# Two-layer decoder trunk: six groups of the MLP through seven products, two plain, and up projections in 512- and 256-column passes

## The chip, the cores and the metric

The kernel runs on one core of a Trainium2 chip. The metric is the device time of one execution in microseconds; below "us" always means that.

## The reference, cut to what matters

The input is 256 positions of 2048 numbers (fp32). Two layers follow, each a token mixer and then an MLP, both behind an RMSNorm and added to the residual x. The change touches the MLP alone:

```python
def squared_relu_mlp(h, w_up, w_down):
    return jnp.square(jax.nn.relu(h @ w_up)) @ w_down
...
        h = rms_norm(x, mlp_norm[layer])
        x = x + squared_relu_mlp(h, w_up[layer], w_down[layer]).astype(x.dtype)
```

Here w_up is 2048 x 8192 and w_down is 8192 x 2048. The norm's scale per position is taken out of the MLP: since relu squared is homogeneous of degree two, the kernel multiplies the MLP's output by the squared scale (the tile rB) at the end.

## The kernel before, in words

**Precision.** Every fp32 operand is split into hi (rounded to the matmul's reduced format) and lo (the rest), and a product is hi by hi, hi by lo and lo by hi. ScalarE makes hi of a weight chunk (L1308) and VectorE lo (L1319), five and four chunks ahead of TensorE. Weights come from HBM in transfers of 1 MB into three buffers named raw, issued on SyncE's queue. The activations stand in the tile xs, for each of 16 K-tiles 256 columns of hi and 256 of lo side by side.

**One stream.** All weight chunks of the kernel are in one list, `stream`, and its order is the order of TensorE's work. A chunk is four K-tiles of 256 weight columns, thus 8 pairs of K-tile and 128-column half (j). A `Block` is the chunks that add up in one PSUM tile: it asks for the tile (`take`) at its first chunk and calls `done` after its last. In `consume` the kind says which passes are made: kind U makes three passes of 256 columns (L467 to L469) and adds everything in one bank; kind T, so far used by the mixers, makes one pass of 512 columns (hi of the weight by hi and lo of the activation, L476) and one of 256 (lo by hi, L477), and its result stands in two halves of two banks that `done` has to add.

**The MLP** (`mlp`) splits the 8192 hidden columns into NGRP = 8 groups of 1024. A group's up projection is nb = 4 blocks of 16 K-tiles. `up_done` empties the bank (relu L1002, square L1006) and leaves jobs that make the tile hs of it. The down projection of groups 0 to 6 goes "through products": for each of four column blocks cb of 512 columns, seven chunks make 29 products where 32 would be plain (seven products in place of eight for three of four block pairs, and the pair named in PLAIN the plain way). Each product is three passes of 256 columns (L497 to L499) into the PSUM tiles s0 and s1, two banks each. ScalarE copies s0 and s1 to the SBUF tile stage, of which there are two (L1116), and GpSimd's queue adds them by DMA to the DRAM tensor sums (L1119, L1121). The stream interleaves products of group g with the up chunks of group g + 1: in each round 7 product chunks (87 passes) and the 4 chunks of one up block, and an up block's end is followed by two product chunks (18 passes) before the next up block.

**The end of an MLP.** After the last round of products `combine` adds the eight quarters of sums among each other by DMA, one column block after the other (L1133), and loads the result to the tile sum (L1137), all on GpSimd's queue, which runs in order. The last group's down projection is plain: 8 blocks of 256 columns with 8 K-tiles each. Before the last chunk of block b `add_sums(b)` turns its part of sum (L1148), scales it and adds it to x; `down_done` adds the block itself (L1160, L1161). In the last layer block 7 has the kind "last", and `final_block` prepares the output block by block with the gain tile (L1232), which GpSimd's queue loads (L982).

**PSUM.** Eight banks: two for side, two each for s0 and s1, and one each for the two tiles named up that hold the U blocks.

## Time and profile before

| what | value |
|---|---|
| median of 3 runs | 2225.75 us (2218.46 to 2233.47) |
| the profiled execution, its own time | 2223.67 us |
| its span in the profile | 2221.9 us |
| TensorE, matmul passes | 2167.8 us busy, 16494 passes |
| TensorE, weight loads | 2087.0 us busy |
| VectorE | 1605.1 us busy |
| ScalarE | 1286.8 us busy |
| DMA | 468.14 MB, 211 GB/s over the span |

How to read it: the passes of TensorE overlap, so a busy TensorE tells only that one of them was in flight, and its rate has to be read from the number of passes in a stretch. The profiled execution took 2 us less than the median, so numbers from it carry over to the median as they are.

### The profile page before, as it was taken

The page shows a single profiled execution, that of the slowest core. Times are in us where ns is not written, and L with a number is a line of the kernel's source. Part 1 is how long each engine was busy: PE and PEld are TensorE (multiplying, and loading weights), DVE is VectorE, ACT ScalarE, POOL GpSimd, SP SyncE. Part 2 cuts the span into 40 slices and gives each one's busy share as a digit, 9 for nine tenths or more (in the row PEclk, how much of TensorE's full clock was granted, in tenths as well). Part 3 has the DMA queues.
Part 4 walks back from the last instruction along what each step waited for, and adds up shares of the span by engine and source line. Part 5 has one row for each costly group of instructions (what it writes and reads, how often), then busy time and mean ns, then how long its engine had stood idle before and what let it go on. Part 6 is the DMA issues. An engine that isn't in the chain of part 4 may idle for free.

```text
span 2221.9 us, 40179 instructions
## 1 busy us (share of the span) xinstructions
PE 2167.8 (98%) x16494; PEld 2087.0 (94%) x16494; DVE 1605.1 (72%) x2145; ACT 1286.8 (58%) x1746; POOL 176.9 (8%) x233
## 2 busy tenths in 40 slices
PE   9999999999999999999699999999999999999987
PEld 7898989999999999998688889989999999999986
DVE  6765666778787878777667665577887878787656
ACT  6554545566667666665355436456666666666552
POOL 0000000000000000023200000000000000000232
PEclk9999999999999999999899999999999999999998
DMA  8545456688989898899754455666788888889995
GB/s 261 175 147 162 152 188 177 193 253 232 244 243 237 248 236 232 236 251 236 186 171 152 142 174 167 162 177 191 245 242 239 238 246 244 238 238 244 249 240 140
DMA packets 307943, 468.14 MB, mean 211 GB/s; under 512 B 12120, under 2 KB 182176, under 8 KB 307760
## 3 DMA queue, kind: packets, MB, share of 16 engines
q1 hardware_dynamic: 280224, 392.32, 57.7%
q0 software_dynamic: 27504, 73.25, 16.3%
q8 instruction: 129, 2.11, 0.4%
q14 instruction: 54, 0.44, 0.1%
q10 hardware_dynamic: 32, 0.01, 0.0%
HBM read 404.73 MB, written 69.21 MB: 213 GB/s over the span
## 4 chain that ended last, share of the span: by engine, by line
issue 46%; PE 39%; DMA 10%; POOL 5%; DVE 0%; ACT 0%; POOLq 0%; SPq 0%; ACTq 0%
PE mm L476 14%; DMA sums<-sums 9%; PE mm L477 8%; POOL sums L1121 3%; PE mm L463 2%; PE mm L461 2%; PE mm L462 2%; PE up L467 2%; PE up L468 2%; PE up L469 2%; PE mm L479 1%; PE side L352 1%; DMA sums<-stage 1%; PE side L375 1%; PE side L421 1%
## 5 line engine op out<-in xcount | busy, mean ns | idle before, releaser
L1308 ACT ACTIVATE hi<-raw 128x1024 fp32r<-128x1024 f32 (+2 forms) x812 | 742.7, 930 | 557.2 <-PE up L468 252.1
L1319 DVE TENSOR_TENSOR lo<-raw,hi 128x1024 fp32r<-128x1024 f32 (+2 forms) x812 | 851.3, 1066 | 286.5 <-ACT hi L1308 104.9
L469 PE MATMUL up<-xs,lo 128*128 128x256 f32 x2048 | 577.3, 282 | 4.4 <-DVE lo L1319 4.4
L468 PE MATMUL up<-xs,hi 128*128 128x256 f32 x2048 | 578.7, 283 | 0.0
L467 PE MATMUL up<-xs,hi 128*128 128x256 f32 x2048 | 577.1, 282 | 1.6 <-DVE xT L758 1.6
L497 PE MATMUL s<-hi,hs 128*128 128x256 f32 x1624 | 456.2, 281 | 0.0
L498 PE MATMUL s<-lo,hs 128*128 128x256 f32 x1624 | 456.0, 281 | 0.0
L499 PE MATMUL s<-hi,hs 128*128 128x256 f32 x1624 | 456.0, 281 | 0.0
L469 PEld LDWEIGHTS up<-xs,lo 128*128 128x128 f32 x2048 | 386.7, 189 | 6.2 <-DVE lo L1319 6.2
L467 PEld LDWEIGHTS up<-xs,hi 128*128 128x128 f32 x2048 | 386.2, 189 | 1.9 <-ACT hi L1308 1.9
L468 PEld LDWEIGHTS up<-xs,hi 128*128 128x128 f32 x2048 | 384.5, 188 | 0.0
L476 PE MATMUL mm<-xs,hi 128*128 128x512 f32 x885 | 319.6, 401 | 1.6 <-DVE t L1160 1.0
L499 PEld LDWEIGHTS s<-hi,hs 128*128 128x128 f32 x1624 | 306.3, 189 | 0.0
L497 PEld LDWEIGHTS s<-hi,hs 128*128 128x128 f32 x1624 | 306.3, 189 | 0.0
L498 PEld LDWEIGHTS s<-lo,hs 128*128 128x128 f32 x1624 | 306.2, 189 | 0.0
L1319 DVE TENSOR_TENSOR lo<-w,hi 128x1024 fp32r<-128x1024 f32 x168 | 205.7, 1224 | 123.3 <-PE up L469 67.7
L477 PE MATMUL mm<-xs,lo 128*128 128x256 f32 x944 | 259.0, 280 | 0.2 <-DVE lo L1319 0.2
L476 PEld LDWEIGHTS mm<-xs,hi 128*128 128x128 f32 x885 | 166.1, 188 | 39.4 <-issue 1.2
L1308 ACT ACTIVATE hi<-w 128x1024 fp32r<-128x1024 f32 x168 | 176.9, 1053 | 37.8 <-DVE w L1068 27.8
L477 PEld LDWEIGHTS mm<-xs,lo 128*128 128x128 f32 x944 | 177.3, 188 | 3.0 <-DVE lo L1319 0.5
L1116 ACT ACTIVATE stage<-s 128x1024 f32<-128x1024 f32 x112 | 114.4, 1021 | 74.5 <-PE s L499 65.4
L1121 POOL DMA_DIRECT2D sums<-stage x96 | 89.1, 1006 | 848.1 <-ACT stage L1116 846.3
(297 smaller groups left out, 2761.7 us busy)
## 6 DMA issues: line engine op xcount, KB each, us to landing
raw<-w_up SPq DMA_DIRECT2D x128, 1024.0 KB, 6.2
raw<-w_down SPq DMA_DIRECT2D x128, 1024.0 KB, 5.5
sums<-stage POOLq DMA_DIRECT2D x112, 512.0 KB, 9.3
raw<-od_w_in SPq DMA_DIRECT2D x36, 1024.0 KB, 5.0
raw<-ev_w_in SPq DMA_DIRECT2D x30, 1024.0 KB, 5.4
raw<-ev_w_out SPq DMA_DIRECT2D x16, 1024.0 KB, 5.0
raw<-od_w_in SPq DMA_DIRECT2D x20, 512.0 KB, 4.9
sums<-sums POOLq DMA_DIRECT2D x64, 128.0 KB, 5.8
```

Source lines behind the costliest of these rows:

```text
L467: mm(ps[:, j], hi[:, n, c], m[:, 0:T], start=first and j == 0, stop=False)
L468: mm(ps[:, j], hi[:, n, c], m[:, T:], start=False, stop=False)
L469: mm(ps[:, j], lo[:, n, c], m[:, 0:T], start=False, stop=last and j == 1)
L476: mm(ps[:, j], hi[:, n, c], m, start=first, stop=False)
L477: mm(ps[:, j, 0:T], lo[:, n, c], m[:, 0:T], start=False, stop=False)
L497: mm(ps, x[:, a, 0:P], hi[:, w], start=(i, o) == bank[0], stop=False)
L498: mm(ps, x[:, a, 0:P], lo[:, w], start=False, stop=False)
L499: mm(ps, x[:, a, P:], hi[:, w], start=False, stop=(i, o) == bank[-1])
L1116: act(stage, ps.rearrange("p b c -> p (b c)"), AF.Copy)
L1121: nc.gpsimd.dma_start(to, stage, accum_op=OP.add)
L1308: act(d, r, AF.Copy)
L1319: tt(d, r, f32(h), op=OP.subtract)
```

## The change

The constant NS = 6 says how many groups go through products; groups 6 and 7 are plain. The up chunks of group 7 follow alone after the last round, and then come the 8 plain down blocks, now with 16 K-tiles each. `combine` starts after the products of group 5. Kind U is gone: up blocks and plain down blocks are of kind T, except the block of kind "last". A T block needs two banks, so there is one tile up (groups 1 to 6 use it, `take_up`), and the up blocks of groups 0 and 7 and the down blocks alternate between s0 and s1 (`take_free`). `up_done` and `down_done` first copy one half of the PSUM tile on ScalarE and add the other on VectorE. The sums of the column blocks 2 and 3 are loaded into the two buffers of stage.

```diff
--- before.py
+++ after.py
@@ -463,11 +463,7 @@
                 mm(o, xl, hi[:, n], start=False, stop=last)
                 continue
             c = slice(j * P, (j + 1) * P)
-            if block.kind == "U":
-                mm(ps[:, j], hi[:, n, c], m[:, 0:T], start=first and j == 0, stop=False)
-                mm(ps[:, j], hi[:, n, c], m[:, T:], start=False, stop=False)
-                mm(ps[:, j], lo[:, n, c], m[:, 0:T], start=False, stop=last and j == 1)
-            elif block.kind == "last":
+            if block.kind == "last":
                 mm(ps[j], hi[:, n, c], m[:, 0:T], start=first, stop=False)
                 mm(ps[j], hi[:, n, c], m[:, T:], start=False, stop=False)
                 mm(ps[j], lo[:, n, c], m[:, 0:T], start=False, stop=last)
@@ -982,7 +978,7 @@
                 nc.gpsimd.dma_start(fn[i], final_norm[c].unsqueeze(0).to_broadcast([P, D // 2]))
             E["fn"] = lambda c0, n: fn[c0 // (D // 2)][:, c0 % (D // 2):c0 % (D // 2) + n]
 
-        NGRP = 8
+        NGRP, NS = 8, 6
         PLAIN = (3,)
         W = FF // NGRP
         nb = W // T
@@ -991,15 +987,21 @@
         hs = {}
 
         def take_up():
-            return st["banks"].tile([P, 2, T], F32, name="up", bufs=2)
+            return banks("up", 1)
+
+        def take_free(b):
+            return lambda: banks(f"s{b % 2}", 1)
 
         def take_last():
-            return [banks(f"s{j}", 1)[:, 0, 0:T] for j in range(2)]
+            ps = banks("s1", 1)
+            return [ps[:, j, 0:T] for j in range(2)]
 
         def up_done(grp, b):
             def f(ps):
                 t = temp()
-                act(t, ps, AF.Relu)
+                act(t, ps[:, :, T:], AF.Copy)
+                tt(t, ps[:, :, 0:T], t, op=OP.add)
+                act(t, t, AF.Relu)
                 if (grp, b) != (0, 0):
                     need(("h", layer) + ((grp, b - 1) if b else (grp - 1, nb - 1)))
                 r = E["pool"].tile([P, 8, P], F32, name="hr", bufs=1)
@@ -1007,7 +1009,7 @@
 
                 def job():
                     h = E["pool"].tile([P, 7, 2 * P], F32R, name="hs", bufs=2 * nb)
-                    if grp == NGRP - 1:
+                    if grp >= NS:
                         h = h.rearrange("p o t -> p (o t)")[:, 0:4 * T].rearrange("p (j t) -> p j t", j=2)
                         split_into(h, r[:, 0:4].rearrange("p (j k) t -> p j (k t)", j=2))
                     elif b in PLAIN:
@@ -1119,7 +1121,7 @@
                     nc.gpsimd.dma_start(to, stage)
                 else:
                     nc.gpsimd.dma_start(to, stage, accum_op=OP.add)
-                if grp == NGRP - 2 and half == "s1":
+                if grp == NS - 1 and half == "s1":
                     jobs.spawn(combine(cb), keys=[("sum", cb)], delay=2)
                     if last and cb == 3:
                         load_gain()
@@ -1132,7 +1134,8 @@
                 for to, src in step:
                     nc.gpsimd.dma_start(to, src, accum_op=OP.add)
                 yield 2, 0
-            g = hs["sum", cb] = E["pool"].tile([P, 2, 2, T], F32, name="sum", bufs=2)
+            g = E["pool"].tile([P, 4 * T], F32, name="sum" if cb < 2 else "stage", bufs=2)
+            g = hs["sum", cb] = g.rearrange("p (a b c) -> p a b c", a=2, b=2)
             for tok, half, src in ((0, 0, p4), (0, 1, p7), (1, 0, p2), (1, 1, p3)):
                 nc.gpsimd.dma_start(g[:, tok, half], src)
             jobs.done.add(("sum", cb))
@@ -1157,7 +1160,9 @@
                 need(("rB", n0))
                 t = temp()
                 rB = E.setdefault("rB", st["rB"])
-                tt(t, ps, rB[:, None, :].to_broadcast([P, 2, T]), op=OP.mult)
+                act(t, ps[:, :, T:], AF.Copy)
+                tt(t, ps[:, :, 0:T], t, op=OP.add)
+                tt(t, t, rB[:, None, :].to_broadcast([P, 2, T]), op=OP.mult)
                 tt(xT[b], xT[b], t, op=OP.add)
                 if last:
                     final_block(E, b)
@@ -1180,8 +1185,8 @@
             return chunks
 
         def up_list(grp):
-            blocks = [Block("U", eights(up, grp * W + b * T, KT), mov, up_done(grp, b), take=take_up)
-                      for b in range(nb)]
+            blocks = [Block("T", eights(up, grp * W + b * T, KT), mov, up_done(grp, b),
+                            take=take_up if 0 < grp <= NS else take_free(b)) for b in range(nb)]
             return [(block, i) for block in blocks for i in range(len(block.chunks))]
 
         def product_list(grp):
@@ -1193,22 +1198,26 @@
             return [(block, i) for block in blocks for i in range(len(block.chunks))]
 
         stream.extend(up_list(0))
-        for grp in range(NGRP - 1):
+        for grp in range(NS):
             s, u = product_list(grp), up_list(grp + 1)
             for i in range(len(u)):
                 a, b = (i // 4 * 7 + (0, 2, 4, 5, 7)[i % 4 + e] for e in range(2))
                 stream.extend(s[a:b] + u[i:i + 1])
 
+        for grp in range(NS + 1, NGRP):
+            stream.extend(up_list(grp))
+
         def h_mov(kt):
-            need(("h", layer, NGRP - 1, kt // 2))
-            return hs[NGRP - 1, kt // 2][:, kt % 2]
-        wd = down[FF - W:]
+            grp, b = NS + kt // (2 * nb), kt // 2 % nb
+            need(("h", layer, grp, b))
+            return hs[grp, b][:, kt % 2]
+        wd = down[NS * W:]
         for b in range(8):
+            w = eights(wd, b * T, (NGRP - NS) * W // P)
             if last and b == 7:
-                add(Block("last", eights(wd, b * T, W // P), h_mov, lambda ps: last_block(E, ps), take=take_last,
-                          extra=add_sums(b)))
+                add(Block("last", w, h_mov, lambda ps: last_block(E, ps), take=take_last, extra=add_sums(b)))
             else:
-                add(Block("U", eights(wd, b * T, W // P), h_mov, down_done(b), take=take_up, extra=add_sums(b)))
+                add(Block("T", w, h_mov, down_done(b), take=take_free(b), extra=add_sums(b)))
         return open_pool, pool_ctx.close
 
 
@@ -1242,7 +1251,7 @@
             tt(t[:, j], ps[j], E["rB"], op=OP.mult)
             tt(xl[:, j], xl[:, j], t[:, j], op=OP.add)
             act(sq[:, j], xl[:, j], AF.Square)
-        sums, turn = banks("s0", 1), side()
+        sums, turn = banks("up", 1), side()
 
         def add_up(a, first, last):
             for tok in range(2):
```

In VectorE's order, where an up block ends between products (raw is a buffer of weights, w_7124 to w_7263 are weight tiles made for the products), the kernel before has these rows:

```order
L1319 TENSOR_TENSOR lo<-raw,hi 128x1024
L1319 TENSOR_TENSOR lo<-raw,hi 128x512
L1319 TENSOR_TENSOR lo<-raw,hi 128x1024
L1319 TENSOR_TENSOR lo<-w_7124,hi 128x1024
L1319 TENSOR_TENSOR lo<-w_7125,hi 128x1024
L1060 TENSOR_TENSOR w_7263<-raw 128x512
```

Nothing of the up block's end stands there, since before ScalarE alone empties the bank. In VectorE's order of the changed kernel the same place reads (w_6890 and w_6891 are made weight tiles again):

```order
L1328 TENSOR_TENSOR lo<-raw,hi 128x1024
L1328 TENSOR_TENSOR lo<-raw,hi 128x512
L1328 TENSOR_TENSOR lo<-raw,hi 128x1024
L1003 TENSOR_TENSOR t<-up,t 128x512
L1328 TENSOR_TENSOR lo<-w_6890,hi 128x1024
L1328 TENSOR_TENSOR lo<-w_6891,hi 128x1024
```

The addition t<-up,t now stands between the lo of the chunk three ahead and that of the chunk four ahead.

In ScalarE's order at this place (stage<-s copies s0 or s1, t<-up empties the up bank, hr<-t squares) the kernel before has:

```order
L1308 ACTIVATE hi<-raw 128x512
L1116 ACTIVATE stage<-s_6968 128x1024
L1308 ACTIVATE hi<-raw 128x1024
L1116 ACTIVATE stage<-s_7036 128x1024
L1308 ACTIVATE hi<-w_7124 128x1024
L1002 ACTIVATE t<-up 128x512
L1006 ACTIVATE hr<-t 128x512
```

The relu that empties the bank comes behind two staged copies and the hi of the chunk four ahead. ScalarE of the changed kernel has there:

```order
L1317 ACTIVATE hi<-raw 128x512
L1118 ACTIVATE stage<-s_6754 128x1024
L1317 ACTIVATE hi<-raw 128x1024
L1118 ACTIVATE stage<-s_6811 128x1024
L1317 ACTIVATE hi<-w_6890 128x1024
L1002 ACTIVATE t<-up 128x512
L1004 ACTIVATE t<-t 128x512
L1008 ACTIVATE hr<-t 128x512
```

One row more stands there: t<-up is now the copy of one half, and the relu, t<-t, comes behind it and waits for VectorE's addition.

In GpSimd's queue at the end of layer 0's products (sums_1_99 to sums_3_101 are the DRAM tensors of the column blocks 1 to 3) the kernel before has, following group 6:

```order
L1133 DMA sums_1_99<-sums_1_99 128x256 x6
L1121 DMA sums_2_100<-stage 128x1024 x2
L1133 DMA sums_1_99<-sums_1_99 128x256 x2
L1137 DMA sum<-sums_1_99 128x256 x4
L1133 DMA sums_2_100<-sums_2_100 128x256 x6
L1121 DMA sums_3_101<-stage 128x1024 x2
L1133 DMA sums_2_100<-sums_2_100 128x256 x2
L1137 DMA sum<-sums_2_100 128x256 x4
L1133 DMA sums_3_101<-sums_3_101 128x256 x8
L1137 DMA sum<-sums_3_101 128x256 x4
```

The staged copies of block 2 stand behind six additions of block 1, those of block 3 behind six of block 2. In GpSimd's queue of the changed kernel, following group 5, stands:

```order
L1135 DMA sums_1_99<-sums_1_99 128x256 x6
L1123 DMA sums_2_100<-stage 128x1024 x2
L1135 DMA sums_1_99<-sums_1_99 128x256 x2
L1140 DMA sum<-sums_1_99 128x256 x4
L1135 DMA sums_2_100<-sums_2_100 128x256 x6
L1123 DMA sums_3_101<-stage 128x1024 x2
L1135 DMA sums_2_100<-sums_2_100 128x256 x2
L1140 DMA stage<-sums_2_100 128x256 x4
L1135 DMA sums_3_101<-sums_3_101 128x256 x8
L1140 DMA stage<-sums_3_101 128x256 x4
```

The order is the same, one group of products earlier, and only the last loads have moved, from sum to stage.

## Rows read from the trace of the kernel before

**Rows 1.** The page: span; TensorE's busy tenths and granted clock in 40 slices.
```profile
span 2221.9 us, 40179 instructions
PE   9999999999999999999699999999999999999987
...
PEclk9999999999999999999899999999999999999998
```

**Rows 2.** Waits of TensorE: who waited for whom; us in total, times, longest us.
```profile
PE side L1148 <- DMA sum<-sums: 17.5, 5, 6.8
PE up L467 <- ACT hs L167: 10.8, 2, 5.7
PE side L1230 <- DVE xs L1232: 5.5, 1, 5.5
PE up L469 <- DVE lo L1319: 4.4, 5, 1.5
...
PE mm L476 <- DVE t L1160: 1.0, 1, 1.0
```

**Rows 3.** Stretches, TensorE: us, busy us (passes), granted clock, DMA share, GB/s.
```profile
1032.80:1039.70 6.90, 5.67 (x25) 0.51 0.86 237
1063.50:1070.40 6.90, 3.49 (x15) 0.51 0.96 215
1084.00:1094.30 10.30, 3.88 (x17) 0.50 0.79 219
2145.60:2152.40 6.80, 4.19 (x18) 0.50 0.93 261
2169.50:2176.30 6.80, 6.02 (x28) 0.50 0.84 235
```

**Rows 4.** The same view of three stretches in which TensorE never pauses.
```profile
320.00:360.00 40.00, 40.00 (x230) 1.00 0.63 194
365.00:405.00 40.00, 40.00 (x337) 1.00 0.64 189
1700.00:1900.00 200.00, 200.00 (x1679) 1.00 0.89 242
```

**Rows 5.** Timeline of TensorE in a product chunk: start us, us, instruction.
```profile
1017.82 0.28 PE L497 MATMUL s<-hi,hs 128*128 128x256 f32 x1
...
1020.67 0.28 PE L497 MATMUL s<-hi,hs 128*128 128x256 f32 x1
```

**Rows 6.** Timeline of GpSimd's queue at the end of layer 0's products.
```profile
1012.82 2.72 POOL L1121 DMA_DIRECT2D sums<-stage  x2
...
1063.34 1.66 POOL L1137 DMA_DIRECT2D sum<-sums  x3 [6.38 <-DMA sums<-sums]
...
1087.73 1.65 POOL L1137 DMA_DIRECT2D sum<-sums  x3 [3.80 <-DMA sums<-sums]
```

**Rows 7.** Timeline of ScalarE there: start us, us, instruction, idle before it.
```profile
1024.11 1.03 ACT L1116 ACTIVATE stage<-s 128x1024 f32<-128x1024 f32 x1 [5.15 <-PE up L469]
```

**Rows 8.** The tile stage between 1005 and 1030 us, its two DMAs.
```profile
DMA to landing us min/median/max: 11.2/12.6/14.0
```

**Rows 9.** Stretches, TensorE, beside the final additions; columns as in rows 3.
```profile
988.00:1010.00 22.00, 20.58 (x173) 1.00 1.00 271
1044.00:1060.00 16.00, 15.87 (x133) 1.00 0.89 186
```

**Rows 10.** Timeline of three engines where an up block ends, between products.
```profile
800.79 0.28 PE L469 MATMUL up<-xs,lo 128*128 128x256 f32 x1
...
801.11 0.60 ACT L1002 ACTIVATE t<-up 128x512 f32<-128x512 f32 x1 [0.47 <-PE up L469]
...
801.18 1.23 DVE L1319 TENSOR_TENSOR lo<-w,hi 128x1024 fp32r<-128x1024 f32 x1 [1.14 <-PE up L469]
...
803.05 0.28 PE L467 MATMUL up<-xs,hi 128*128 128x256 f32 x1
```

**Rows 11.** Groups of VectorE: busy us, mean ns of one, idle before.
```profile
L337 DVE TENSOR_TENSOR t<-mm,t 128x512 f32<-128x512 f32 x11 | 7.6, 692 | 16.6 <-ACT t L334 16.6
```

## The prediction

> **What bounds the kernel now.** I read the page's slices first, then the waits of TensorE, then stretches, then timelines where a wait ends. In the slices TensorE is at 9 tenths nearly everywhere; one slice in the middle, where the MLP of layer 0 ends, falls to 6, and the last two fall to 8 and 7 [rows 1]. So two things set the time: the rate at which passes follow each other, and the ends of the two MLPs.
>
> The waits name what happens at the ends [rows 2]: 17.5 us for the loads of sum, 10.8 us for the last hs, 5.5 us for the gain tile, 1.0 us for a bank at the start of the next mixer. Together 34.8 us. The 4.4 us for lo belong to the stretch ahead of the ends and are kept apart.
>
> A second price hangs on these waits. Five stretches, all within the ends, show a granted clock of 0.50 or 0.51, the level of 1.2 GHz; the clock fell after TensorE had stood for some microseconds, and the lo waits, of 1.5 us at most, are followed by no fall [rows 2, 3]. In the fullest of the five, 28 passes take 6.02 us, 215 ns each, where a pass at full clock takes 119 (below). The five hold 25 + 15 + 17 + 18 + 28 = 103 passes, and 103 x 96 ns = 9.9 us are lost in them.
>
> For the rate, a stretch's passes are counted less two that reach over its edges [rows 4]. A mixer with T blocks: 228 passes, 114 pairs in 40 us, 350.9 ns for a pair of 512 and 256 columns. Up blocks of kind U: 335 passes, 111.7 triples in 40 us, 358.2 ns. Eight triples of a product chunk take 2.85 us, 356.2 ns [rows 5]. Beside products 1677 passes take 200 us, so a round of 96 U and 87 product passes takes 21.82 us; less 29 x 0.3562 that leaves 359.2 ns for a U triple, about what it takes alone. TensorE is thus the bound in the groups, and a saved pass is saved time.
>
> **Part 1, passes.** The same columns in two passes in place of three save 358.2 - 350.9 = 7.3 ns per K-tile and half. Up has 2 x 1024 of these: -15.0 us. The plain group that exists already has 240 outside the block of kind "last": -1.8 us.
>
> The Trainium skill, "TensorE: Matmul & The Clock Gate", section "Wait — 56ns, not 53.3ns?", has a fixed cost of about 2.5 ns per warm pass on top of its columns; by that the saving would be 2.5 x 2288 = 5.7 us in place of 16.8, and the sum 11 us higher. The trace has 7.3 for the pass saved and decides.
>
> **Part 2, one group more is plain.** It loses the eighth that the products save. In each layer 4 x 29 product triples go, 116 x 356.2 = 41.3 us, and 128 plain pairs come, 128 x 350.9 = 44.9 us: +3.6 us a layer, +7.2 in all. VectorE loses the weight sums and hs splits of a group per layer, GpSimd's queue eight staged copies; neither was waited for in the groups, so that is counted at nothing. Passes together: -9.6 us.
>
> **Part 3, the ends.** Before, the plain down blocks come straight after the products, and the final additions run behind the kernel: in layer 0 the products end at 1021 us, the loads for column block 2 are issued at 1063 and those for block 3 at 1088 [rows 5, 6], landing some microseconds on, and block b = 6 stands and waits. After, between the end of the products and the first sum come the four up blocks of group 7, 4 x 32 x 0.351 = 45 us, and each down block takes 11.2 us in place of 5.7. Block 4 needs its sum some 45 + 5 x 11.2 = 101 us after the products, block 6 some 123 us; the loads are issued 42 and 67 us after them. The cover is over 50 us, so the 17.5 us go, even if the additions take half as long again. The gain tile is wanted 59 us after the products in place of 9, so its 5.5 us go too. The last hs is now the sixteenth K-tile of the first down block and has some 10 us where it had 4. The bank wait goes because the next mixer's first bank is now s0, which block 6 left one block earlier. With no stand of several microseconds left, the 9.9 us of half clock go as well. All: -34.8 - 9.9 = -44.7 us.
>
> One thing stays and moves. The hs wait had a cause behind it: ScalarE stood 5.15 us before a staged copy [rows 7], because both buffers of stage were still on their way; their DMAs took 11.2 and 14.0 us [rows 8] and had been issued at 1013 behind the additions of the block ahead [rows 6]. The row names the up block's last pass, but 1012.82 + 11.2 is 1024.0, just ahead of the copy's start at 1024.11. That queue is in the same order after, so the jam comes again, now ahead of group 7's up blocks. The first of these wants s0, which the late copy frees at 1025.1; TensorE would come for it at 1023.8. I put 1.4 us a layer for this, +2.8; it is nothing if the copies come earlier, and 5.4 a layer if hi is as late as hs was. The 4.4 us for lo have the same cause and are left in.
>
> **Part 4, one pair of banks.** Where an up block ends beside products, the next one must now wait until ScalarE has copied one half (0.60 us) and VectorE added the other (0.692 us) [rows 10, 11]. The last pass ends at 801.07, the copy starts 0.04 us later, and the next up pass is at 803.05, 18 product passes on [rows 10]: 1.98 us of cover for 1.3 to 1.4 us of work. The lo that VectorE did at 801.18 comes behind the addition now and is wanted three chunks later. So 0.6 us is left and the cost is nothing; with a lo of 1.23 us in front of the addition, the next block would wait some 0.6 us at each of 48 such places. The copy and the addition cost ScalarE 0.6 and VectorE 0.7 us per block of 21.8, beside work. The 15 down blocks have the other bank pair as cover; the last one of layer 0 delays x, which the next mixer wants for the last of its 16 K-tiles.
>
> **Sum.** 2223.7 (the profiled execution) - 9.6 - 44.7 + 2.8 = 2172.2 us. That execution stands 2 us under the median, less than the runs spread, so I take 2172.
>
> **The rivals.** (1) Starved TensorE: the additions now run beside weights at full rate. Before, at a DMA share of 1.00 TensorE had 20.58 of 22 us, at 0.89 it had 15.87 of 16 [rows 9]. If the 67 us of additions after the products are all like the first, 6.5% of them are lost, 4.4 us a layer, and one fall of the clock in each (25 x 96 ns) makes 6.8: 2172 + 13.6 = 2186. For it: transfers of the plain group beside the additions. Against: the second of these rows is such a stretch, and it is fed.
>
> (2) The merged pass saves nothing beside products: T pairs are seen only at a DMA share of 0.63, products run at 0.89 [rows 4]. Then the 6 x 128 x 2 = 1536 pairs of groups 1 to 6 bring none of their 7.3 ns: +11.2, 2183. Against: U is as fast beside products as alone. The page's fixed cost, above, would come to the same time.
>
> (3) Slower: the bank pair sets the pace. If the addition comes late at each of the 48 places by 0.6 us and the clock falls there each time (25 passes x 96 ns = 2.4 us), 48 x 3.0 = 144 us are lost: 2316. From 1.07 us a place on it is slower than before (51.5 / 48). For it: VectorE has a lo just ahead of the addition in its order. Against: VectorE stood idle 1.14 us before 801.18 [rows 10], and stands of 1.5 us lowered no clock [rows 2, 3]. The same without the clock gives 2172 + 29 = 2201. The Trainium skill, "TensorE: Matmul & The Clock Gate", section "A second HAM failure mode: psum-queue depth-cycling", tells of such a kernel, whose clock fell and rose because of short pauses between bank groups; no stretch of this trace shows that.
>
> **How the numbers follow.** The forecast 0.72; (1) 0.10; (2) 0.10; (3) without the clock 0.05, with it 0.03. A measurement of this kernel can tell about 1% from no change, here 2203.5 us: the first four lie below, by little in the fourth. Faster 0.94, same 0.03, slower 0.03. Range: downward, the lo waits going too (4.4), no jam (2.8) and U at 359.2 beside products (1.5) give 2163, and the runs before spread by 8: 2154. Upward 2186 and the same spread: 2194.
>
> **What would show it.** Up: passes of 512 and 256 columns, 351 ns a pair, alone and beside products. No wait for sum, gain or the last hs, and the clock at full from the first products to the tail. A short wait for s0 or hi at the first up block of group 7. No wait for up at the 48 places. Wrong would be: rows of up waiting for VectorE's addition, waits for raw in group 7, or a clock of 0.5 within the groups.

## The result and the profile after

| kernel | median us (range, runs) | ratio to before |
|---|---|---|
| before | 2222.8 (2218.5 to 2233.5, 4) | 1 |
| changed | 2198.9 (2195.6 to 2204.1, 4) | 0.9888 (0.9845 to 0.993) |

The change gains 24 us where 52 were forecast. The profiled execution of the changed kernel took 2204.07 us, 5 above its median. Its page, which answers to [rows 1]: the slices at the end of layer 0's MLP no longer fall, nor does the granted clock there.

```profile
span 2202.3 us, 35006 instructions
PE   9999999999999999999999999999999999999998
...
PEclk9999999999999999999999999999999999999999
```

TensorE's waits, which answer to [rows 2] (us in total, times, longest): sum, gain, the last hs and the mixer's bank are gone. In their place stand waits of up and of group 7 (its blocks use s) for lo, for the addition t, for hi and for the copy into stage.

```profile
PE up L473 <- DVE lo L1328: 8.2, 9, 3.3
PE up L472 <- DVE t L1003: 6.9, 14, 1.0
PE s L472 <- ACT stage L1118: 5.6, 2, 4.2
PE up L472 <- ACT hi L1317: 4.1, 2, 2.7
```

Stretches of TensorE, columns as in [rows 3] and [rows 4]:

```profile
427.00:513.24 86.24, 86.24 (x606) 1.00 0.75 244
...
600.00:800.00 200.00, 197.07 (x1361) 1.00 0.86 236
...
900.00:993.00 93.00, 85.99 (x521) 0.98 0.97 252
...
916.60:920.00 3.40, 3.40 (x12) 0.50 0.82 115
2008.80:2012.20 3.40, 3.40 (x12) 0.50 0.50 131
2046.40:2049.80 3.40, 3.40 (x11) 0.50 1.08 360
```

A round is one up block with seven product chunks, 64 + 87 = 151 passes. The first row holds four rounds (604 passes and two over the edges): 21.56 us each. The prediction's terms give 32 x 0.3509 + 29 x 0.3562 = 21.56 us. At that rate 200 us hold 1401 passes; the second row has 1361, so 40 passes or 5.7 us are missing, though the stretch shows only 2.9 us in which TensorE was not busy. The loss is thus larger than the waits that are listed. The third row is the end of layer 0's products and the up blocks of group 7. The last three are what is left of the half clock, 10.2 us in place of 37.7; TensorE had stood 3.3 us just ahead of the first of them, 2.7 and 0.8 us ahead of the second, 4.2 us ahead of the third.

So the rate is as forecast in the first rounds of each layer and is lost later, and the ends lose time again, in another place. What changed between the rounds is seen in the list of waits of ScalarE, which turns raw weights into hi. Before, then after (us, times, longest):

```profile
ACT hi L1308 <- DMA raw<-w_up: 31.8, 12, 6.1
```

```profile
ACT hi L1317 <- DMA raw<-w_up: 185.3, 75, 11.0
```

The loads of w_up come late. To see why, take the second round of layer 0, where nothing is late yet. Timelines of VectorE, SyncE's queue and GpSimd's queue in the kernel before (start us, us, instruction, idle before it):

```profile
445.93 1.22 DVE L1319 TENSOR_TENSOR lo<-raw,hi 128x1024 fp32r<-128x1024 f32 x1
447.48 0.69 DVE L1319 TENSOR_TENSOR lo<-raw,hi 128x512 fp32r<-128x512 f32 x1 [0.33 <-PE s L498]
...
448.20 0.37 SPq L1174 DMA_DIRECT2D raw<-w_up  x1
...
448.85 0.53 POOL L1119 DMA_DIRECT2D sums<-stage  x1 [19.43 <-ACT stage L1116]
```

The same place in the changed kernel:

```profile
445.77 1.82 DVE L1328 TENSOR_TENSOR lo<-raw,hi 128x1024 fp32r<-128x1024 f32 x2
...
447.62 0.37 SPq L1179 DMA_DIRECT2D raw<-w_up  x1
...
447.09 0.53 POOL L1121 DMA_DIRECT2D sums<-stage  x1 [19.18 <-ACT stage L1118]
```

The 0.69 us lo is the last reader of a raw buffer, and the w_up load goes into that buffer. Before, VectorE was ahead of TensorE there (idle 0.33 us), and the load was issued 0.65 us ahead of the staged copy's DMA, which is released by the end of the same product chunk. After, VectorE does both lo without a pause, and the load is issued 0.53 us behind that DMA. What holds it back lies 19 us earlier, where the up block ends. In the lists of waits from 410 to 530 us VectorE waits there for ScalarE's copy of the up half, 1.6 us a time, and then adds for 0.69 us; ScalarE waits for that addition before its relu.

```profile
DVE t L1003 <- ACT t L1002: 8.2, 5, 1.6
...
ACT t L1004 <- DVE t L1003: 3.8, 5, 0.8
```

The next hi stands behind this chain. It starts 2.56 us after the copy (431.01 and 428.45), where before it started 1.18 us after the relu (431.18 and 430.00). Its lo is late by the same 1.4 us, and from there VectorE works without a pause up to the lo that frees the buffer.

How long the load takes, by the tile raw, issued at 448.20 before, and at 447.62 and 533.85 after:

```profile
DMA to landing us min/median/max: 6.8/6.8/6.8
```

```profile
DMA to landing us min/median/max: 8.4/8.4/8.4
...
DMA to landing us min/median/max: 11.6/11.6/11.6
```

The first of the late ones falls into a round that writes the sums (group 0), the second into one that adds to them. It is so in both layers up to the final additions: loads issued ahead of the staged DMA take 6.2 to 8.1 us in the changed kernel, those behind one that writes 7.2 to 8.5, those behind one that accumulates 10.6 to 14.3. Some rounds on, hi stands for raw. ScalarE at 1666 us of the changed kernel, where the load had been issued at 1655.07, 1.61 us behind the staged DMA, and took 11.2 us:

```profile
1666.37 1.89 ACT L1317 ACTIVATE hi<-raw 128x1024 fp32r<-128x1024 f32 x3 [2.88 <-DMA raw<-w_up]
```

### The profile page after: what moved, and what is told of

Read it like the earlier page. It is cut to its first block, busy times and chain, and to the rows that moved or that the text cites. A ratio compares the mean times of both kernels' runs of the same rounds, so it can differ in the third digit from the quotient of the medians.

```text
span 2202.3 us, 35006 instructions
## 1 busy us (share of the span) xinstructions
PE 2159.3 (98%) x14038; PEld 1953.4 (89%) x14038; DVE 1588.7 (72%) x2120; ACT 1284.6 (58%) x1777; POOL 162.6 (7%) x217
## 4 chain that ended last, share of the span: by engine, by line
PE 58%; issue 22%; DMA 13%; DVE 3%; POOL 2%; ACT 2%; SPq 0%; POOLq 0%; ACTq 0%; DVEq 0%
PE mm L472 14%; PE mm L473 8%; DMA raw<-w_up 7%; PE s L472 6%; DMA sums<-sums 5%; PE up L472 5%; PE s L473 3%; PE up L473 3%; DVE lo L1328 2%; PE s L493 2%; PE s L494 2%; PE s L495 2%; PE mm L461 2%; PE mm L463 2%; PE mm L462 2%
## 5 line engine op out<-in xcount | busy, mean ns | idle before, releaser
L1317 ACT ACTIVATE hi<-raw 128x1024 fp32r<-128x1024 f32 (+2 forms) x804 | 738.9, 942 | 506.5 <-DMA raw<-w_up 185.3
L472 PE MATMUL up<-xs,hi 128*128 128x512 f32 x1440 | 522.6, 399 | 11.1 <-DVE t L1003 6.9
L473 PE MATMUL up<-xs,lo 128*128 128x256 f32 x1536 | 428.1, 284 | 9.4 <-DVE lo L1328 8.2
L494 PE MATMUL s<-lo,hs 128*128 128x256 f32 x1392 | 390.6, 281 | 0.0
L493 PE MATMUL s<-hi,hs 128*128 128x256 f32 x1392 | 390.5, 281 | 0.0
L495 PE MATMUL s<-hi,hs 128*128 128x256 f32 x1392 | 390.3, 280 | 0.0
L472 PEld LDWEIGHTS up<-xs,hi 128*128 128x128 f32 x1440 | 271.8, 189 | 70.9 <-DVE t L1003 10.4
L473 PEld LDWEIGHTS up<-xs,lo 128*128 128x128 f32 x1536 | 290.5, 189 | 22.2 <-DVE lo L1328 19.6
L493 PEld LDWEIGHTS s<-hi,hs 128*128 128x128 f32 x1392 | 262.3, 188 | 6.5
L495 PEld LDWEIGHTS s<-hi,hs 128*128 128x128 f32 x1392 | 262.4, 188 | 0.0
L472 PE MATMUL s<-xs,hi 128*128 128x512 f32 x480 | 171.5, 398 | 8.3 <-ACT stage L1118 5.6
L1317 ACT ACTIVATE hi<-w 128x1024 fp32r<-128x1024 f32 x144 | 150.9, 1048 | 19.2 <-DVE w L1070 15.8
L472 PE MATMUL s<-hs,hi 128*128 128x512 f32 x450 | 161.0, 398 | 0.0
L473 PE MATMUL s<-xs,lo 128*128 128x256 f32 x512 | 141.5, 281 | 1.2 <-DVE lo L1328 1.2
```

Source lines behind the costliest of these rows:

```text
L472: mm(ps[:, j], hi[:, n, c], m, start=first, stop=False)
L473: mm(ps[:, j, 0:T], lo[:, n, c], m[:, 0:T], start=False, stop=False)
L493: mm(ps, x[:, a, 0:P], hi[:, w], start=(i, o) == bank[0], stop=False)
L494: mm(ps, x[:, a, 0:P], lo[:, w], start=False, stop=False)
L495: mm(ps, x[:, a, P:], hi[:, w], start=False, stop=(i, o) == bank[-1])
L1317: act(d, r, AF.Copy)
```

## The experiments

Theory **A**: VectorE's addition turns the order of two transfers round, and a w_up load that is issued behind an accumulating DMA lands late; that costs the groups their rate. Theory **B**, the prediction's third rival: the single pair of banks does it. For the ends, **Q**: the final additions stand in GpSimd's queue ahead of the last staged copies; **D**: they slow the weight loads wherever they run. Of all kernels this table tells the time, the ratio to the kernel before on the same chip, and ScalarE's total wait for w_up in the profiled execution. e2 and e3 have two runs each, the others at least four.

| kernel | us | ratio (95%) | hi for w_up, us |
|---|---|---|---|
| changed | 2198.9 | 0.9888 (0.9845 to 0.993) | 185.3 |
| e1_u_in_groups | 2192.8 | 0.9831 (0.9773 to 0.9889) | 157.5 |
| e2_u_with_chain | 2207.4 | 0.9897 (0.981 to 0.9983) | 182.7 |
| e3_no_accumulate | 2169.0 | 0.9724 (0.9638 to 0.981) | 49.9 |
| e4_stage_after_load | 2195.4 | 0.9845 (0.9779 to 0.9911) | 42.5 |
| e5_stage_pair | 2183.7 | 0.9819 (0.9776 to 0.9861) | 59.1 |
| e6_additions_last | 2202.3 | 0.9899 (0.9863 to 0.9934) | 187.3 |
| e7_t_alone | 2233.7 | 1.0043 (1.0018 to 1.0068) | 172.4 |
| e8_pair_and_last | 2182.4 | 0.9809 (0.976 to 0.9858) | 32.2 |
| e9_one_column_block | 2162.3 | 0.9711 (0.9682 to 0.974) | 12.2 |
| e10_no_final_additions | 2161.8 | 0.9709 (0.9675 to 0.9744) | 11.9 |
| e11_hs_on_gpsimd | 2190.9 | 0.9841 (0.9808 to 0.9875) | 154.4 |
| e12_one_block_alone | 2181.9 | 0.9796 (0.9749 to 0.9843) | 171.5 |

**Bank pair or order.** e1 puts kind U with its two small banks back into groups 1 to 6; e2 does the same but keeps a copy, a VectorE step and a relu behind it.

```
# e1
+            return st["banks"].tile([P, 2, T], F32, name="up", bufs=2)
...
+                if 0 < grp <= NS:
+                    act(t, ps, AF.Relu)
# e2
+                    act(t, ps, AF.Copy)
+                    tt(t, t, t, op=OP.max)
+                    act(t, t, AF.Relu)
```

> Groups 1 to 6 of the changed kernel get back the up blocks of before: three passes of 256 columns, two tiles up of one bank, relu straight from the bank. Everything else is as changed. In the changed kernel a round (one up block and 7 product chunks) takes 22.2 us and most loads of w_up that are issued beside the staged copies land in 11 to 12 us; before it was 21.8 us and 7 us. Theory A (VectorE's addition makes the release of a raw buffer late, so that a load of w_up is issued behind the staged addition instead of 0.65 us ahead of it, lands 5 us later, and ScalarE, the emptying of up and TensorE wait for it): loads ahead again, rounds of 21.8, time about 2199 - 48 x 0.4 = 2180 us. Theory B (the one pair of banks alone costs the time, since copy and addition take longer than the two product chunks): rounds of 21.8 too, 2180. Theory C (the loss has nothing to do with the up blocks): 2199.

> As the run with U in groups 1 to 6, but the up bank is emptied by the same chain of work as in the changed kernel: copy on ScalarE, an operation of the same size on VectorE (max of the tile with itself), relu. The bank is free after the copy and there are two, so no up block can wait for VectorE. Theory A: the load of w_up falls behind the staged addition again in three of four rounds, lands in 11 to 12 us, rounds of about 22.2 us, time near 2199. Theory B: rounds of 21.8 us, time as with U alone, about 2180.

With two banks and the chain (e2) the kernel is 14.6 us slower than with two banks and no chain (e1). In e1 the w_up load stays ahead of the staged DMA for 10 rounds of layer 0 and 13 of layer 1. In e2 it is behind from the second round on (0.39 us, where e1 is 0.65 us ahead), as in the changed kernel. The banks are the same in both, so it is the chain that turns the order round, by A. That it also costs the 14.6 us is not shown. e1 too falls behind in the end and misses A's 2180 by 13 us, and in the profiled executions the rounds 2 to 21 take 424 us in e1 and 423 in e2 in layer 0, 420 and 427 in layer 1; more than half of the difference lies at the ends. The order is not stable in any kernel of this form, the kernel before included: in its last seven rounds of layer 0 the load is 0.6 to 2.5 us behind and takes 11.4 to 12.8 us.

**The accumulating DMA.** e3 writes the staged copies over the sums of the group before (it leaves out the addition over groups); e4 and e5 keep the addition and change the order: both staged DMAs go out together, e4 behind a one-element read of the block's last lo, e5 behind a one-element read of the second stage tile.

```
# e3
+                nc.gpsimd.dma_start(to, stage)
# e5 (e4: the copy reads the block's last lo)
+                if half == "s0":
+                    E["late"] = to, stage
+                    return
+                look = tmp.tile([P, 1], F32, name="look", bufs=2)
+                nc.gpsimd.tensor_copy(look, stage[:, 0:1])
+                for a, b in (E["late"], (to, stage)):
...
+                        nc.gpsimd.dma_start(a, b, accum_op=OP.add)
```

> The changed kernel with the staged copies written over sums instead of added (it leaves out the addition over groups). The order of the issues stays, w_up behind the staged copy, but in the rounds of group 0, which write, such loads landed in 8.5 us and no round lost time. Theory A: rounds of 21.6 us, 48 x 0.6 = 30 us less, about 2170. Theory B: rounds of 22.2, about 2199.

> The changed kernel, but both staged additions of a round are issued together behind a copy of one element per partition on GpSimd that waits for the lo which releases the raw buffer; so the load of w_up is issued ahead of them. Nothing else changes. Theory A: these loads land in about 7 us, rounds of 21.6 us, and the time falls by about 30 us to 2170, the forecast. Theory B: rounds of 22.2 and 2199. If the release of the raw buffer is itself too late, whatever the order of issues: 2185 to 2199, with waits for raw left.

> The changed kernel, but both staged additions of a round are issued together behind a copy of one element per partition on GpSimd that waits for the second staged copy, some 2 us later than the first is issued now; so the load of w_up is ahead of them by about 1.4 us. In the run that let GpSimd look at lo all rounds but the last ones took 21.74 us, 0.18 more than the 21.56 of rounds without loss. Theory A (the order of the two issues costs the time in the groups): rounds of 21.56 up to the last two or three of each layer; the end of the products is still late, as the final additions stand ahead of staged copies; about 2175 to 2185 us. If it is not the order but VectorE's lateness that starves TensorE: rounds of 22 and more, 2199.

In e3 the order stays turned round in most rounds (the load at 1660.77, the staged DMA at 1660.25), but the load lands in 7.2 us there, in 7.1 to 9.6 in all such rounds ahead of the final additions, and the rate holds up to these. The view of stretches, and the load by the tile raw:

```profile
1700.00:1900.00 200.00, 200.00 (x1404) 1.00 0.76 247
```

```profile
DMA to landing us min/median/max: 7.2/7.2/7.2
```

The bank pair, the addition and the copy are all still in e3, so B has nothing left to explain: they cost the groups no time by themselves. (e3 does wait for the addition twice, 9.1 us in all, in the last rounds, beside the final additions.) In e5 the load is ahead by 1.1 to 2.8 us in every round of the groups and lands in 5.3 to 7.7 us until the last rounds. Its rate is 1391 passes in 200 us, steady to the end but not 1401: rounds of 21.74 us, in e4 and in all later kernels with the pair as well. No wait stands behind these 0.18 us a round, the product passes are a little longer (119.5 ns from start to start in e9, below, against 118.0 in the changed kernel, in the mean of the four rounds from 427 us); why stays open. e4 has the rounds of e5 and loses part of its gain again at the end of layer 1, 7 us more there than the changed kernel; so it misses A's 2170.

```profile
1700.00:1900.00 200.00, 200.00 (x1391) 1.00 0.89 242
```

**The ends.** e6 takes the final additions away from the last rounds and starts all four column blocks side by side behind them; e8 does this to e5. e9 does it to e5 with one column block after the other, e12 does so to the changed kernel; e10 is e5 without the additions (it leaves them out and loads the sums as they are).

```
# e6, e8
+                    for c in range(4 * (cb == 3)):
+                        jobs.spawn(combine(c), keys=[("sum", c)], delay=2)
# e9, e12
+                    if cb == 3:
+                        jobs.spawn(combine_all(), keys=[("sum", c) for c in range(4)], delay=2)
...
+        def combine_all():
+            for c in range(4):
+                yield from combine(c)
# e10
-                for to, src in step:
-                    nc.gpsimd.dma_start(to, src, accum_op=OP.add)
```

> The changed kernel, but the final additions of all four column blocks start only after the last round of products, side by side; no staged copy stands behind them in GpSimd's queue. Between the start of the last full round and the first down block the changed kernel loses about 10 us in layer 0 and 13 in layer 1. Theory Q (the queue's order: staged copies behind additions that wait for each other, so stage, s0 and ScalarE come late): these 23 us shrink to about 3 to 5, the groups stay as they are, 2199 - 20 = 2179. Theory D (the additions take DMA time from the loads of weights wherever they run): the loss moves into group 7 and the down blocks, time 2190 to 2199.

> Both edits together: staged additions of a round issued as a pair behind the second copy, final additions after the last round of products. If theories A and Q hold and the two losses are separate: 24 us of the groups and about 20 us of the ends, 2199 - 44 = 2155 us. If the loss only moves from one place to the other: 2175 or more.

> The kernel e5_stage_pair (2183.7 us), with the final additions of all four column blocks behind the last round, one column block after the other (in e8_pair_and_last the four ran side by side, in e5_stage_pair each behind its own staged copies). Theory D, that the additions cost the weight loads time wherever they run: still about 2183, with the last rounds normal and the time lost in group 7's up blocks and the down blocks, as in e8_pair_and_last (gap 51.9 and 52.7 us where 47.8 is undisturbed). Rival, that it is their crowding that costs: about 2175, with gaps near 48 us.

> The kernel e5_stage_pair (2183.7 us) without its final additions: the sums of the groups are only loaded, not added over the lists (leaves out that part of the computation). Theory D, that these additions slow the weight loads at the two ends: the last round of each layer 21.7 us in place of 28.5 and 22.0, the gap from the last product to the first down pass 47.8 us in both layers in place of 50.7 and 55.1, together about 17 us less, 2166. Rival, that the ends lose their time to the staged copies of the last blocks: the gap and the last rounds stay and the time stays at 2180 to 2184.

> The changed kernel (2198.9 us) with the final additions behind the last round, one column block after the other, and the staged additions as they are: the second half of what made e9_one_column_block 21 us faster than e5_stage_pair. If the two causes are separate, the loss in the groups stays (rounds of 22 to 23 us from the eighth on, the w_up load behind the staged addition) and the end is put right (last rounds below 23 us, gap from the last product to the first down pass about 48 us where the changed kernel has 52.8 and 53.8): 2175 to 2180. Rival, that the end is late because the groups hand it late w_up loads: the gap stays over 51 us and the time at 2190 to 2200.

e6 makes the last rounds normal and loses the time behind them, and e8 gains nothing on e5 (2182.4 and 2183.7 us). By its expectation that speaks against Q, but e6 and e8 also do what the changed kernel never does: they have the additions of all four column blocks under way together. In the changed kernel's queue those of a block are issued when those of the block ahead have landed, and the staged copies stand between them:

```profile
913.25 1.65 POOL L1140 DMA_DIRECT2D sum<-sums  x3 [7.31 <-DMA sums<-sums]
914.89 1.75 POOL L1135 DMA_DIRECT2D sums<-sums  x2
...
927.86 2.47 POOL L1135 DMA_DIRECT2D sums<-sums  x3 [4.34 <-DMA sums<-sums]
929.43 2.71 POOL L1123 DMA_DIRECT2D sums<-stage  x2
```

The stretch of e6 in which the additions run, and the tile raw from 925 to 990 us:

```profile
900.00:993.00 93.00, 84.79 (x504) 0.97 1.02 260
935.00:985.00 50.00, 44.43 (x246) 1.00 1.14 253
```

```profile
DMA to landing us min/median/max: 5.6/16.7/20.6
```

The loads land in 16.7 us (median) while GpSimd issues six and then nine additions in a row. That spoke for D. D is wrong: e9 differs from e8 only in that the column blocks follow each other, so that the same additions are spread over more time, and takes 2162.3 us, within 0.5 us of e10, which has none. Nor is it the staged copies alone, since e10 still has these. So it is not the additions as such that cost e6 and e8 their 20 us, but how many are under way at once. e9's list of waits has no row for up, the tile sum or hs (one load of sums into stage is waited for, 1.1 us), and its loads at the end land in 6.8 us in the median. TensorE's waits, the stretch, and the tile raw from 895 to 990 us (changed kernel: 11.0, ScalarE waiting 31.5 us):

```profile
PE s L472 <- DVE xT L754: 1.6, 1, 1.6
PE mm L210 <- DVE ones L186: 1.2, 1, 1.2
PE side L1162 <- DMA stage<-sums: 1.1, 1, 1.1
```

```profile
900.00:993.00 93.00, 93.00 (x572) 1.00 0.91 241
```

```profile
  ACT hi L1328: 7.1, 7
...
DMA to landing us min/median/max: 5.2/6.8/12.4
```

e12 completes the square: the changed kernel with its additions behind the last staged copies, one column block at a time. Its groups lose as before (hi stands 171.5 us for w_up) and its end of layer 0 does not; its profile, the slowest of five runs (2190.9 us), still has 3.9 us of waits for sums and 6.8 us of half clock at the end of layer 1.

```profile
900.00:993.00 93.00, 92.87 (x577) 1.00 0.92 248
...
935.00:983.00 48.00, 48.00 (x276) 1.00 0.99 260
```

What e12 takes away is the mixture of staged DMAs and additions. In the changed kernel three additions and two staged DMAs are issued from 892 to 897 us; the staged ones take 12.8 and 15.6 us (7.1 and 9.8 for that pair in e12), and a w_down load issued at 901.76 takes 11.9 us (5.4 in e12, at 901.85). ScalarE waits 7.8 us for that load, and TensorE's 3.3 us ahead of the half clock follow from it. The stands of 2.7 and 4.2 us go back to w_up loads in the same way (ScalarE waits 8.2 and 11.0 us for them); only 1.4 us in layer 0 go back to a staged copy that is late, as Q has it. The tile raw from 895 to 990 us, changed kernel and e12:

```profile
DMA to landing us min/median/max: 5.9/11.0/17.8
```

```profile
DMA to landing us min/median/max: 5.3/7.3/14.0
```

Q's order of the queue thus matters in that it puts these DMAs beside each other. Whether fewer at a time in the old order would do as well was not tried.

| us | additions between the staged copies (as changed) | behind them, one column block at a time |
|---|---|---|
| staged DMA as changed | 2198.9 | 2181.9 |
| staged DMAs as a pair | 2183.7 | 2162.3 |

The order in the groups is worth 15.2 or 19.6 us, the place of the additions at the ends 17.0 or 21.4, both 36.6. In none of these pairs do the runs overlap, and each step is worth about the same with and without the other: the two are separate causes. The sizes are rough, since the four kernels ran on different chips; by the ratios in the table above they are 15 or 19, 20 or 24, and 39 us. e9 is faster than both kernels, 2.9% under the kernel before.

**Parts of the change, and VectorE.** e7 is the change with seven product groups, so that the products and the end of the kernel before remain; e11 is the changed kernel with one subtraction of hs on GpSimd.

```
# e7
+        NGRP, NS = 8, 7
# e11
-                        tt(h[:, :, P:], r[:, 1:8], f32(h[:, :, 0:P]), op=OP.subtract)
+                        nc.gpsimd.tensor_tensor(h[:, :, P:], r[:, 1:8], f32(h[:, :, 0:P]), op=OP.subtract)
```

> The changed kernel with seven groups through products, as before (NS = 7): the new up and down passes alone, without the group that became plain. By my prediction's terms: 16.8 us less than before, stands at the ends kept: about 2206. By theory A 20 or so of the 56 rounds lose 0.6 us each in each layer, 25 us, and the ends keep their stands: about 2225 to 2235, no gain over before.

> The changed kernel with one subtraction of the hs of the blocks with products moved from VectorE to GpSimd, nothing else. Theory A, that VectorE's backlog makes the w_up load come behind the staged addition in the queues: VectorE is lighter by about 1 us in three of four rounds, the w_up load is issued ahead of the staged addition again (by some 0.5 us, as in the kernel before), it lands in some 7 us in place of 11 to 13, and the rounds stay at 21.6 us for most of the groups: 2175 to 2185. Rival, that VectorE's load does not matter and the additions slow the loads anyway: 2195 to 2200, rounds as in the changed kernel. If GpSimd is late with hs or its queue with the staged copies, a wait for hs shows and the time is over 2200.

e7 is 0.4% slower than before: the cheaper passes alone lose more by the order than they gain, and the waits at the ends stay (sum 17.2, hs 16.0, gain 6.1 us). All of the gain of the change thus came with the plain group. e11 is no test of A, since its premise failed: VectorE did not get lighter. 36 subtractions of 1.085 us left it, but the 620 large lo rose from 1221 to 1328 ns, 66 us in all, since a lo beside GpSimd's subtraction takes longer. The groups of e11, GpSimd and VectorE (busy us, mean ns):

```profile
L1028 POOL TENSOR_TENSOR hs<-hr,hs 128x896 fp32r<-128x896 f32 x36 | 90.4, 2511 | 906.4 <-PE s L473 381.9 <-PE s L472 284.7 <-ACT hs L1026 130.7
```

```profile
L1328 DVE TENSOR_TENSOR lo<-raw,hi 128x1024 fp32r<-128x1024 f32 x620 | 816.9, 1328 | 217.7 <-ACT hi L1317 75.2 <-PE mm L473 70.5 <-PE mm L462 36.2
```

The load stayed some 1.2 us behind and landed in 8 to 13 us, and ScalarE waited 154.4 us for it. Yet the groups lost little: TensorE waits for nothing there, and its passes come nearly as in e5.

```profile
600.00:800.00 200.00, 199.91 (x1387) 1.00 0.86 243
1700.00:1900.00 200.00, 199.71 (x1387) 1.00 0.86 240
```

So a load that is issued late and lands late is not the whole price: its rounds take 21.83 us with a lag (of the load behind the staged DMA) that stays near 1.2 us, those of the changed kernel 22.2 with one that goes from 0.5 to 2.5. What makes the difference is open. The time is 8 us under that of the changed kernel, with intervals that overlap; in the profiled executions 13.5 of the 15.8 us between the two lie in the rounds of the groups. A kernel in which VectorE has really less to do was not tried. That the chain turns the order round rests on e1 against e2 and on the timelines; that the order, with an accumulating DMA, costs the time rests on e3, e4 and e5.

## Why the prediction was wrong

**Right.** Part 1: a T pair takes 351 ns beside products as well; 21.56 us a round is the sum of the terms, and e1 with kind U has 671 passes in 80 us at the same place, 21.82 us for a round of 183. The 32 passes saved thus bring 0.26 us, 8 ns each, where 7.3 were forecast. That ends the second rival; the 2.5 ns per pass that the Trainium skill states ("TensorE: Matmul & The Clock Gate", section "Wait — 56ns, not 53.3ns?") would have made 0.08 us; the measured 0.26 decides. Part 2's passes are in that sum. Part 3: the waits for sum, gain, the last hs and the bank went, by the cover that was named. Part 4, the bank itself: 14 waits for the addition, 1.0 us at most, 6.9 in all, and none in the groups of e3; ahead of the final additions no stretch of the groups lost its clock. The third rival did not happen.

**The step that failed, in the groups.** "The copy and the addition cost ScalarE 0.6 and VectorE 0.7 us per block of 21.8, beside work", counted at nothing, with the lo behind the addition "wanted three chunks later". I asked when TensorE wants that lo, and not how far the delay runs on. The chain of copy, addition and relu made the next hi 1.4 us late, VectorE had no pause in which to catch up, and 19 us on a lo that is the last reader of a raw buffer ended late; its end issues the next w_up load. That load moved from 0.65 us ahead of the staged DMA to 0.53 us behind it. Measured price of this order: 15 to 20 us in place of 0 (not of the order alone, as e11 shows). The prediction's list of signs named rows of up waiting for the addition, and such rows came, but as a small part of the loss.

**The term that was mis-sized, at the ends.** The jam was put at +2.8 us, a late copy ahead of group 7, 1.4 us a layer. In layer 0 that wait came as put, 1.4 us. The ends lost 17 to 21 us all the same, by a term that the sum has not: staged DMAs and additions were under way together, weight loads took 11.0 us in the median and 17.8 at most, and TensorE stood for them. The clock fell three times, where Part 3 had the half clock gone: 35 passes, at 96 ns 3.4 us. The first rival, additions beside weights at full rate, came nearest with 13.6 us, but such additions by themselves cost 0.5 us (e9 against e10). That its 2186 lay between forecast and result is luck.

**The sum.** Of the 36.6 us that both causes cost, 2.8 and 4.4 (the lo waits left in) were in the forecast: 29.4 were not. The result is 26.9 above the forecast.

## What to carry to other kernels

When an instruction is added to an engine, look not only for who waits for its successors but for which buffers they free: the load that is issued there can change places with another transfer, and then the price is that transfer's. Of several accumulating DMAs, issue few at a time when weights stream beside them: the same additions cost some 20 us with four column blocks side by side (e8) and less than 1 us one block after another (e9). A change that wins in one place may show less than its worth until what it stirs up is put in order: 24 us as made, 65 us (2227.7 to 2162.3 on the same chip) with two edits to the order of DMAs. How much of the 65 us belongs to the change is not shown: the two edits were not tried on the kernel before, which also has late loads in its last rounds and staged copies between additions.

## What was not expected of the hardware

- A 1 MB load takes 6.8 us when it is issued 0.65 us ahead of a 512 KB DMA, 11.6 us when it is issued some 0.5 us behind one that accumulates (10.6 to 14.3 over the changed kernel's groups), and 7.1 to 9.6 us behind one that only writes (e3).
- In the changed kernel the lag grows from round to round: 0.53, 1.61 and 2.12 us in three rounds of layer 1, up to 2.5 elsewhere. A late load makes hi and lo late, and with them the next load. In e11 it does not grow.
- GpSimd's 128 x 896 subtraction takes 2.51 us where VectorE's takes 1.085, and lengthens what VectorE does beside it: some 1.8 us for each, e11 against the changed kernel.
